# Second sweep of a hybrid GLA/MLA encoder layer: the gated output turned by VectorE and DMA, and a float32 state product

## The chip, the cores and the metric

The kernel runs on one core of a Trainium2 chip. A core has five engines that work side by side, each through its own queue in order: TensorE (PE; its weight loads are listed as PEld), VectorE (DVE), ScalarE (ACT), GpSimd (POOL) and SyncE (SP), which issues most of the DMAs. Sixteen DMA engines move the data. The metric is the device time of one execution, in microseconds; before the change the median of three runs is 1285.17 us (1284.21 to 1286.22).

## The reference

One layer over 2048 rows of width 1024, all in float32. The input is projected once; the columns feed a group of gated linear attention (GLA, 4 heads, key width 64, value width 128) and a group of latent attention (MLA, 4 heads). The two outputs (512 + 512) go through one output projection and a residual LayerNorm. What matters here is the GLA group's end:

```python
o_fwd = gla_chunked(q, k, v, log_af, strict=False)
o_bwd = flip(gla_chunked(flip(q), flip(k), flip(v), flip(log_ab), strict=True))
o = rms_norm(o_fwd + o_bwd, norm_g)          # per head, over 128 values
o = o.reshape(B, S, D_GLA).astype(gate.dtype)
return o * jax.nn.silu(gate)
...
return jnp.concatenate([o_a, o_b], axis=-1) @ w_out
```

In chunked form a chunk's output is a part within the chunk plus the decayed queries times a state that runs over the chunks: `o = o_intra + q_dec @ state`. The forward state runs up through the chunks, the backward one down.

## The kernel before

The rows are cut into 16 chunks of 128. Three stages follow one another.

The first sweep (`sweep_a`) goes from the last chunk to the first. It projects q, k, v and the decays, and computes per chunk the part within the chunk, the decayed queries of both directions stacked on 128 partitions (64 forward, 64 backward), the state update of the forward direction and the finished state of the backward one. Four tiles per chunk go to memory: `qd_s` (queries), `oi_s` (part within the chunk), `su_s` (forward update in partitions 0 to 63, backward state in 64 to 127) and `u_s` (the SiLU gate). From its fifth chunk on, this sweep turns q and k by VectorE in 32x32 blocks and by four DMAs each (`turn`, L824 to L827); its first chunks turn them on TensorE.

The second sweep (`sweep_c`) goes from the first chunk to the last in 8 steps of two chunks. It makes the MLA projections (`ipm`, `pz`, `pq`, `pqr`) and finishes the GLA output. For each chunk it loads the four tiles (`c_lS`, `c_lq`, `c_lo`, `c_lu`; tiles SU, qdb, oib, ub), carries the forward state `Sf` along on GpSimd (`c_Sf1`, `c_Sf2`) and puts the decayed forward state into the lower half of SU (`c_M`), so that one product of contraction 128 adds both directions. That product (`c_Ob`) is written with split operands: ScalarE rounds qdb and SU to fp32r (`c_qhb`, `c_MMh`), GpSimd forms the rests (`c_qlb`, `c_MMl`), and TensorE multiplies, per head, the queries' high part by both parts of the state (256 columns, L1465) and their low part by the state's high part (128 columns, L1466). VectorE adds the second half of that result to oib (`c_oia`) and both to the first (`c_oib`). ScalarE squares, VectorE forms the scale of the norm and multiplies by it and by the gate (`c_og`). TensorE turns the four heads (`c_ot`), ScalarE takes them out of PSUM with the norm's weight as a scale per partition (`c_oT`, gn_c), and SP stores the chunk to `oa_s` (`c_soT`), 128 partitions of 2 KB.

Attention and the output projection come last (`attention`, `OutProj`). Attention goes over 16 pairs of a head and a block of 512 queries. The eight row blocks of w_out are loaded to `raw`, rounded on ScalarE (`split_hi`, L1875) and their rests formed on GpSimd (`split_lo`); the first four blocks, which multiply the GLA half, are handled in blocks 9 to 12 of attention.

The order of the second sweep is written out by hand: `PLACE_C` gives each operation a place in units of one step (two values where the even and the odd chunk of a step differ), with own tables for the first and the last step. Operations are sorted by it, and each engine, SP included, goes through its own in that order (`in_order`). A tile with `bufs=2` has two buffers; who writes the third waits for the readers of the first. DMAs are readers too. The pool `tr` holds PSUM tiles for transposes, of which `ot`, `tm`, `pqr` and `tq` take turns in two buffers; `gp` holds those of `Ob`, `pz` and `pq`.

Of the kernel before, what the change touches and what calls it, by code (L numbers as in the profile page):

```python
# [18 lines left out]
P = 128  # L19
S = 2048  # L20
D = 1024
NK = D // P
NCH = S // P
H = 4
# [106 lines left out]
STEP_C = ("gm1", "gm2", "gm3", "gm4", "sgm", "pq", "qah", "qal", "sqa", "sqr")  # L131
CHUNK_C = ("lx", "xh", "xl", "lS", "lq", "lo", "lu", "sqm", "ssm", "rml", "rmd", "cq", "ckv", "krf", "krfa",
    "krsh", "krsl", "vh", "vl", "tm", "cqTh", "cqTl", "ckvTh", "ckvTl", "krT", "pqr", "qrf", "qrfa",
    "tq", "qrTh", "qrTl", "Sf1", "Sf2", "M", "qhb", "qlb", "MMh", "MMl", "Ob", "oia", "oib", "sqO",
    "ss", "rgl", "rgd", "og", "ot", "oT", "soT")

FETCH_C = ("lx", "xh", "xl")

# [12 lines left out]
    qhb=(-0.048, 0.321),  # L151
    MMh=(-0.034, 0.412),
    sqO=(0.272, 0.988),
    rgl=(0.283, 1.029),
    sqm=(0.14, 0.858),
# [11 lines left out]
    oia=(0.235, 0.863),  # L167
    ss=(0.278, 1.005),
    rgd=(0.359, 1.067),
    og=(0.391, 1.102),  # L170
# [11 lines left out]
    qlb=(-0.043, 0.428),  # L182
    MMl=(0.004, 0.597),
    krfa=(0.262, 0.862),
    krsl=(0.456, 1.044),
    vl=(0.859, 1.227),
# [38 lines left out]
    Ob=(0.066, 0.896),  # L225
    tm=(0.445, 1.143),
    pqr=(0.716, 1.336),
    tq=(1.11, 1.512),
    ot=(1.009, 1.378),
    xh=(-0.3, 1.403),  # L230
    qhb=(-0.513, 0.421),
    MMh=(-0.164, 0.444),
    sqO=(0.469, 0.999),
    rgl=(0.603, 1.027),
    sqm=(0.073, 0.865),
# [11 lines left out]
    oia=(0.316, 0.899),  # L247
    ss=(0.596, 1.015),
    rgd=(0.636, 1.064),
    og=(0.804, 1.171),  # L250
# [11 lines left out]
    qlb=(-0.023, 0.63),  # L262
    MMl=(-0.109, 0.558),
    krfa=(-0.119, 0.94),
    krsl=(0.252, 1.09),
    vl=(0.627, 1.365),
# [24 lines left out]
    Ob=(0.0, 0.299),  # L291
    tm=(0.495, 1.083),
    pqr=(0.749, 1.284),
    tq=(0.919, 2.161),
    ot=(0.915, 1.082),
    xh=(-0.262, -0.109),
    qhb=(-0.096, 0.079),
    MMh=(-0.13, 0.094),
    sqO=(0.15, 0.374),
    rgl=(0.229, 0.457),  # L300
    sqm=(0.101, 0.657),
# [11 lines left out]
    oia=(0.01, 0.311),  # L313
    ss=(0.166, 0.454),
    rgd=(0.332, 0.461),
    og=(0.336, 0.508),
# [11 lines left out]
    qlb=(-0.062, 0.166),  # L328
    MMl=(-0.068, 0.195),
    krfa=(0.255, 0.636),  # L330
    krsl=(0.395, 0.879),
    vl=(0.968, 2.242),
# [6 lines left out]
    soT=(1.09, 2.304),  # L339
# [21 lines left out]
class K:  # L361
# [765 lines left out]
    def sweep_c(self):  # L1127


        with ExitStack() as ctx:  # L1130
            self.w1 = ctx.enter_context(self.tc.tile_pool(name="wk2", bufs=1, reuse_waits="tile"))
            self.sm = ctx.enter_context(self.tc.tile_pool(name="smc", bufs=2, reuse_waits="tile"))
            chunks = [dict(c=c, j=c % 2, st=c // 2) for c in range(NCH)]
            steps = [dict(st=st, ch=chunks[2 * st:2 * st + 2]) for st in range(NCH // 2)]
            for d in chunks:
                d["step"] = steps[d["st"]]
            Sf = self.w1.tile([64, H, P], F32, tag="Sf", name="Sf", bufs=2)
            self.nc.vector.memset(Sf, 0.0)
            self.Sf = Sf
            todo = []  # L1140

            def put(n, st, fn, *a, j=None):
                last = st == len(steps) - 1
                p = PLACE_C[n]
                p = (last and PLACE_C_LAST.get(n)) or (not st and PLACE_C_FIRST.get(n)) or p
                todo.append((st + (p if j is None else p[j]), len(todo), fn, a))

            for n in SETUP_C:
                put(n, 0, getattr(self, "su_" + n))
            for s in steps:  # L1150
                for n in range(8):
                    put("pz", s["st"], self.c_pz, s, n, j=n)
                for n in STEP_C:
                    put(n, s["st"], getattr(self, "c_" + n), s)
            for d in chunks:
                for n in range(4):
                    put("ip" + "abcd"[n], d["st"], self.c_ip, d, n, j=d["j"])
                for n in CHUNK_C:
                    if (d["st"] or n not in FETCH_C) and (d["c"] < NCH - 1 or n not in ("Sf1", "Sf2")):
                        put(n, d["st"], getattr(self, "c_" + n), d, j=d["j"])  # L1160
            last = dict(self.tail)
            for _, _, fn, a in sorted(todo, key=lambda e: e[:2]):
                with self.in_order(last):
                    fn(*a)


    def su_lset(self):
        nc, ins, w1 = self.nc, self.ins, self.w1
        self.gq = self.bc.tile([P, 2], F32, name="gq")
        self.gkv_b = w1.tile([P, H, P], F32, tag="oT", name="gkv_b")[:, 0]  # L1170
# [259 lines left out]
    def c_Sf1(self, d):  # L1430

        d["Sf"], self.Sf = self.Sf, self.w1.tile([64, H, P], F32, tag="Sf", name=f"Sf{d['c']}", bufs=2)
        cw = self.cw[0:64, d["c"]]
        self.nc.gpsimd.tensor_tensor(self.Sf, d["Sf"], cw[:, 2, :, None].to_broadcast([64, H, P]), ALU.mult)

    def c_Sf2(self, d):
        self.nc.gpsimd.tensor_tensor(self.Sf, self.Sf, d["SU"][0:64], ALU.add)

    def c_M(self, d):

        cw = self.cw[0:64, d["c"]]
        self.nc.gpsimd.tensor_tensor(d["SU"][0:64], d.get("Sf", self.Sf), cw[:, 0, :, None].to_broadcast([64, H, P]),
                                     ALU.mult)

    def c_qhb(self, d):
        d["qh"] = self.w1.tile([P, H, P], F32R, tag="qhb", name=f"qhb{d['c']}")
        self.hi(d["qh"], d["qdb"])

    def c_qlb(self, d):
        d["ql"] = self.w1.tile([P, H, P], F32R, tag="qlb", name=f"qlb{d['c']}")  # L1450
        self.lo(d["ql"], d["qdb"], d["qh"], "pool")

    def c_MMh(self, d):
        d["MM"] = self.w1.tile([P, 2, H, P], F32R, tag="MMb", name=f"MMb{d['c']}")
        self.hi(d["MM"][:, 0], d["SU"])

    def c_MMl(self, d):
        self.lo(d["MM"][:, 1], d["SU"], d["MM"][:, 0], "pool")

    def c_Ob(self, d):  # L1460
        mm = self.nc.tensor.matmul
        t = self.gp.tile([P, H, 2, P], F32, tag="gp", name=f"Ob{d['c']}")
        d["Ob"], d["Ob1"], d["rp"] = t[:, :, 0], t[:, :, 1], t[:, 0, 1]
        for h in range(H):
            mm(t[:, h], d["qh"][:, h], d["MM"][:, :, h], start=True, stop=False)  # L1465
            mm(t[:, h, 0], d["ql"][:, h], d["MM"][:, 0, h], start=False, stop=True)  # L1466

    def c_oia(self, d):
        self.nc.vector.tensor_tensor(d["oib"], d["Ob1"], d["oib"], ALU.add)

    def c_oib(self, d):
        self.nc.vector.tensor_tensor(d["Ob"], d["Ob"], d["oib"], ALU.add)
# [19 lines left out]
            self.nc.vector.scalar_tensor_tensor(d["og"][:, h], d["Ob"][:, h], d["rg"][:, h:h + 1], d["ub"][:, h],  # L1492
                                                ALU.mult, ALU.mult)

    def c_ot(self, d):
        d["ot"] = self.tr.tile([P, H, P], F32, tag="tr", name=f"ot{d['c']}")
        for h in range(H):
            self.nc.tensor.transpose(d["ot"][:, h], d["og"][:, h], self.ident)

    def c_oT(self, d):  # L1500
        d["oT"] = self.w1.tile([P, H, P], F32, tag="oT", name=f"oT{d['c']}")
        self.nc.scalar.activation(d["oT"], d["ot"], AF.Copy, scale=self.gn_c[:, 0:1])

    def c_soT(self, d):
        self.nc.sync.dma_start(self.oa_s[d["c"]], d["oT"])

    def rope(self, dst, src, c, n):

# [342 lines left out]
class OutProj:  # L1851
# [211 lines left out]
```

## Time and profile before

| | |
|---|---|
| median of the runs shown | 1285.17 us (1284.21 to 1286.22) |
| profiled execution, own time | 1286.1 us |
| its span | 1284.3 us |
| TensorE clock granted over the span | 0.998 |
| matmuls | 7050 |
| the four transposes of `ot` | 64 in all, from 385.8 to 590.6 us |
| matmuls of `Ob` | 128 in all, from 369.0 to 570.9 us |
| DMA queue of SP (q1) | 127584 packets, 151.86 MB, 38.4% of 16 engines' span |

Times within the profile count from the start of the span. A row of the chain of waits gives a start, a length and what ran; a row of a group gives line, engine, operation, result <- operands, shapes, count, then busy time and mean ns of one, then the engine's idle time just before it and what ended most of that. A line can be that of a helper (L371 rounds, L377 forms a rest, L425 to L427 are a split product).

### The profile page before, as it was taken

Reading aid. Unit: us, or ns where it says so; the run is one execution under the profiler, and the core shown is the slowest. Engines: PE = TensorE matmul, PEld = TensorE weight load, DVE = VectorE, ACT = ScalarE, POOL = GpSimd, SP = SyncE. Lnnn points to the kernel's source line nnn. Section 1 sums busy time; section 2 is a strip of 40 time slices with the busy share of each in tenths; the row PEclk is TensorE's granted clock in tenths of the full one; section 3 lists DMA queues with packets and bytes.
Section 4 is the critical chain, followed back from the end, with each engine's and each line's share of the span. In section 5 each row is a group of like instructions: output and inputs, shape, how many; then the busy total and the mean of one; then the engine's idle time right before and its main releaser. Section 6 shows DMA issues by size and latency. Waiting matters only on the chain.

```text
span 1284.3 us, 19837 instructions
## 1 busy us (share of the span) xinstructions
PE 1259.7 (98%) x7050; PEld 1109.9 (86%) x7050; DVE 899.4 (70%) x1602; ACT 755.5 (59%) x1230; POOL 761.1 (59%) x476
## 2 busy tenths in 40 slices
PE   7999999999999999999999999999999999999997
PEld 7999999999889999999788888888888888887886
DVE  6635554544575555554888888888888888479997
ACT  7544343444565655555788888888888888511110
POOL 0132323222367666650498888889999999944541
PEclk9999999999999999999999999999999999999999
DMA  8223444444755666547201111111133110375752
GB/s 293 78 79 108 115 111 114 115 105 126 255 171 184 205 205 210 194 149 228 76 1 42 41 42 50 46 54 58 58 89 93 41 42 9 123 227 193 220 189 99
DMA packets 135746, 155.25 MB, mean 121 GB/s; under 512 B 43510, under 2 KB 86142, under 8 KB 135648
## 3 DMA queue, kind: packets, MB, share of 16 engines
q1 hardware_dynamic: 127584, 151.86, 38.4%
q0 software_dynamic: 672, 2.10, 0.4%
q8 instruction: 56, 0.92, 0.4%
q10 hardware_dynamic: 7392, 0.03, 0.3%
q14 instruction: 42, 0.34, 0.2%
HBM read 100.43 MB, written 53.51 MB: 120 GB/s over the span
## 4 chain that ended last, share of the span: by engine, by line
PE 82%; DMA 5%; DVE 4%; ACT 2%; issue 2%; POOL 2%; SPq 2%; DVEq 0%; POOLq 0%; ACTq 0%
PE pz L1237 6%; PE ipm L1308 5%; PE o L425 4%; PE o L426 4%; PE o L427 4%; PE pS L1569 4%; PE pS L1570 4%; PE pS L1572 4%; PE pS L1571 4%; PE pS L1573 4%; PE ipa L425 4%; PE ipa L427 4%; PE ipa L426 4%; PE ipg L427 2%; PE ipg L425 2%
## 5 line engine op out<-in xcount | busy, mean ns | idle before, releaser
L377 POOL TENSOR_TENSOR pl<-s,ph 128x1024 fp32r<-128x1024 f32 x128 | 306.4, 2411 | 57.7 <-ACT ph L371 53.8
L1591 DVE TENSOR_TENSOR rm<-pS,rm 128x512 f32<-128x512 f32 x210 | 144.8, 689 | 36.7 <-ACT s L1578 31.5
L1578 ACT ACTIVATE s<-pS 128x1024 f32<-128x1024 f32 x128 | 131.2, 1026 | 61.8 <-PE pS L1573 52.0
L1615 DVE TENSOR_TENSOR s<-s,mb 128x1024 f32<-128x1024 f32 x128 | 151.2, 1212 | 8.9 <-PE mb L1609 8.2
L371 ACT ACTIVATE ph<-s 128x1024 fp32r<-128x1024 f32 x128 | 135.1, 1057 | 16.9 <-PE o L427 16.4
L1619 ACT ACTIVATE s<-s 128x1024 f32<-128x1024 f32 x128 | 131.4, 1050 | 12.2 <-DVE s L1615 12.1
L425 PE MATMUL ipa<-wah,xah 128*128 128x384 f32 (+1 forms) x384 | 129.7, 338 | 5.5 <-ACT wah L371 5.5
L426 PE MATMUL ipa<-wal,xah 128*128 128x384 f32 (+1 forms) x384 | 124.5, 324 | 0.5 <-DVE wal L377 0.5
L427 PE MATMUL ipa<-wah,xal 128*128 128x384 f32 (+1 forms) x384 | 124.4, 324 | 0.0
L1569 PE MATMUL pS<-qh,ckvT_h 128*128 128x512 f32 x256 | 102.7, 401 | 2.0 <-ACT s L1578 1.2
L1072 POOL TENSOR_TENSOR Sb<-Sb,Us 64x512 f32<-64x512 f32 x15 | 20.9, 1394 | 136.9 <-DVE Us L1064 127.8
L425 PE MATMUL o<-ph,vh 128*128 128x512 f32 x256 | 101.0, 395 | 0.0
L1570 PE MATMUL pS<-ql,ckvT_h 128*128 128x512 f32 x256 | 100.0, 391 | 0.0
L1572 PE MATMUL pS<-rh,krs 128*128 128x512 f32 x256 | 99.9, 390 | 0.0
L1571 PE MATMUL pS<-qh,ckvT_l 128*128 128x512 f32 x256 | 99.9, 390 | 0.0
L1573 PE MATMUL pS<-rl,krs 128*128 128x512 f32 x256 | 99.8, 390 | 0.0
L427 PE MATMUL o<-ph,vl 128*128 128x512 f32 x256 | 99.7, 389 | 0.0
L426 PE MATMUL o<-pl,vh 128*128 128x512 f32 x256 | 99.6, 389 | 0.0
L1642 DVE TENSOR_TENSOR ap<-ap,s 128x512 f32<-128x512 f32 x120 | 83.1, 693 | 2.7 <-ACT s L1619 0.7
L377 POOL TENSOR_TENSOR xal<-xaf,xah 128x1024 fp32r<-128x1024 f32 x12 | 29.7, 2477 | 87.8 <-ACT xah L371 87.8
L377 POOL TENSOR_TENSOR ol<-of,oh 128x512 fp32r<-128x512 f32 x32 | 43.2, 1352 | 62.6 <-ACT oh L371 61.9
L425 PEld LDWEIGHTS ipa<-wah,xah 128*128 128x128 f32 x384 | 72.9, 190 | 7.8 <-ACT wah L371 5.5
(308 smaller groups left out, 3595.6 us busy)
## 6 DMA issues: line engine op xcount, KB each, us to landing
xcf<-xT_dram SPq DMA_DIRECT2D x16, 512.0 KB, 5.1
xr<-x_dram SPq DMA_DIRECT2D x16, 512.0 KB, 6.4
out_dram<-rr SPq DMA_DIRECT2D x32, 256.0 KB, 2.2
xaf<-xT_dram SPq DMA_DIRECT2D x14, 512.0 KB, 4.2
oib<-oi_s SPq DMA_DIRECT2D x16, 256.0 KB, 4.0
qdb<-qd_s SPq DMA_DIRECT2D x16, 256.0 KB, 4.0
SU<-su_s SPq DMA_DIRECT2D x16, 256.0 KB, 4.1
ub<-u_s SPq DMA_DIRECT2D x16, 256.0 KB, 4.2
```

What stands on the lines that cost most here:

```text
L371: return nc.scalar.activation(dst, src, AF.Copy).ins
L377: return e.tensor_tensor(dst, src, hi.bitcast(F32), ALU.subtract).ins
L425: mm(out, ah, bh, start=start, stop=False)
L426: mm(out, ah, bl, start=False, stop=False)
L427: mm(out, al, bh, start=False, stop=stop)
L1569: mm(ps[:, e], kh, qh, start=True, stop=False)
L1570: mm(ps[:, e], kh, ql, start=False, stop=False)
L1571: mm(ps[:, e], kl, qh, start=False, stop=False)
L1572: mm(ps[:, e], kr, rh, start=False, stop=False)
L1573: mm(ps[:, e], kr, rl, start=False, stop=True)
L1591: V.tensor_tensor(d["rm"], src[:, e], d["rm"], ALU.max)
L1615: V.tensor_tensor(s, s, d["mb"][:, None, :].to_broadcast([P, 2, QB]), ALU.subtract)
```

## The change

All of it stands in the second sweep, but for one line in the output projection.

- The state product takes qdb and SU as they are, in float32: four matmuls of 128 columns per chunk. The rounding and the rests (`c_qhb`, `c_qlb`, `c_MMh`, `c_MMl`) and the add `c_oia` are gone.
- The gated output is turned by VectorE in 32x32 blocks straight behind `c_og` (`c_oT`); `c_ot` is gone, and so is ScalarE's eviction. Four DMAs per chunk put the blocks in their places in `oa_s`, each from 32 partitions in runs of 32 values. oT has two buffers instead of one.
- The norm's weight moves from that eviction to w_out: ScalarE scales the first four raw blocks in place.
- The state tile is not cleared: chunk 0 copies its update on GpSimd and clears the lower half of its SU there.
- In the tables, oT moves from (0.998, 1.347) to (0.392, 1.103) in the steady steps, and the odd chunk's store from 1.736 to 1.45. In the last step the store keeps its places.

```diff
@@ PLACE_C @@
-    ot=(0.926, 1.312),
...
-    oT=(0.998, 1.347),
+    oT=(0.392, 1.103),
...
-    soT=(1.119, 1.736),
+    soT=(1.119, 1.45),
@@ PLACE_C_FIRST @@
-    oT=(1.14, 1.433),
+    oT=(0.805, 1.172),
...
-    soT=(1.342, 1.538),
+    soT=(1.342, 1.45),
@@ PLACE_C_LAST @@
-    oT=(1.011, 1.153),
+    oT=(0.337, 0.509),
@@ sweep_c @@
-            Sf = self.w1.tile([64, H, P], F32, tag="Sf", name="Sf", bufs=2)
-            self.nc.vector.memset(Sf, 0.0)
-            self.Sf = Sf
+            self.Sf = None
@@ c_Sf1, c_Sf2, c_M @@
-        self.nc.gpsimd.tensor_tensor(self.Sf, d["Sf"], cw[:, 2, :, None].to_broadcast([64, H, P]), ALU.mult)
+        if d["c"]:
+            self.nc.gpsimd.tensor_tensor(self.Sf, d["Sf"], cw[:, 2, :, None].to_broadcast([64, H, P]), ALU.mult)
...
-        self.nc.gpsimd.tensor_tensor(self.Sf, self.Sf, d["SU"][0:64], ALU.add)
+        if d["c"]:
+            self.nc.gpsimd.tensor_tensor(self.Sf, self.Sf, d["SU"][0:64], ALU.add)
+        else:
+            self.nc.gpsimd.tensor_copy(self.Sf, d["SU"][0:64])
...
+        if not d["c"]:
+            return self.nc.gpsimd.memset(d["SU"][0:64], 0.0)
@@ c_qhb, c_qlb, c_MMh, c_MMl, c_oia, c_ot: removed @@
@@ c_Ob @@
-        t = self.gp.tile([P, H, 2, P], F32, tag="gp", name=f"Ob{d['c']}")
-        d["Ob"], d["Ob1"], d["rp"] = t[:, :, 0], t[:, :, 1], t[:, 0, 1]
+        t = self.gp.tile([P, 2, H, P], F32, tag="gp", name=f"Ob{d['c']}")
+        d["Ob"], d["rp"] = t[:, 0], t[:, 1, 0]
         for h in range(H):
-            mm(t[:, h], d["qh"][:, h], d["MM"][:, :, h], start=True, stop=False)
-            mm(t[:, h, 0], d["ql"][:, h], d["MM"][:, 0, h], start=False, stop=True)
+            self.nc.tensor.matmul(t[:, 0, h], d["qdb"][:, h], d["SU"][:, h], start=True, stop=True)
@@ c_oT @@
-        d["oT"] = self.w1.tile([P, H, P], F32, tag="oT", name=f"oT{d['c']}")
-        self.nc.scalar.activation(d["oT"], d["ot"], AF.Copy, scale=self.gn_c[:, 0:1])
+        f2 = lambda t: t.rearrange("p h t -> p (h t)")
+        d["oT"] = self.w1.tile([P, H, P], F32, tag="oT", name=f"oT{d['c']}", bufs=2)
+        self.nc.vector.transpose(f2(d["oT"]), f2(d["og"]))
@@ c_soT @@
-        self.nc.sync.dma_start(self.oa_s[d["c"]], d["oT"])
+        t = d["oT"].rearrange("p h (a t) -> p h a t", a=4)
+        dst = self.oa_s[d["c"]].rearrange("(a r) h (b t) -> b r h a t", a=4, b=4)
+        for b in range(4):
+            self.nc.sync.dma_start(dst[b], t[32 * b:32 * b + 32])
@@ OutProj.split_hi @@
         wh = self.w_tile("h", k)
+        if k < NK // 2:
+            self.nc.scalar.activation(self.raw[k], self.raw[k], AF.Copy, scale=self.k.gn_c[:, 0:1])
         self.k.hi(wh, self.raw[k])
```

More of the change, by code (lines that the diff above doesn't have):

```diff
@@ L133 @@
     "krsh", "krsl", "vh", "vl", "tm", "cqTh", "cqTl", "ckvTh", "ckvTl", "krT", "pqr", "qrf", "qrfa",
-    "tq", "qrTh", "qrTl", "Sf1", "Sf2", "M", "qhb", "qlb", "MMh", "MMl", "Ob", "oia", "oib", "sqO",
-    "ss", "rgl", "rgd", "og", "ot", "oT", "soT")
+    "tq", "qrTh", "qrTl", "Sf1", "Sf2", "M", "Ob", "oib", "sqO",
+    "ss", "rgl", "rgd", "og", "oT", "soT")
 FETCH_C = ("lx", "xh", "xl")
@@ L181 @@
     Sf2=(-0.48, 0.285),
-    qlb=(-0.043, 0.428),
-    MMl=(0.004, 0.597),
     krfa=(0.262, 0.862),
@@ L261 @@
     Sf2=(-0.613, -0.022),
-    qlb=(-0.023, 0.63),
-    MMl=(-0.109, 0.558),
     krfa=(-0.119, 0.94),
@@ L327 @@
     Sf2=(-0.624, 1.82),
-    qlb=(-0.062, 0.166),
-    MMl=(-0.068, 0.195),
     krfa=(0.255, 0.636),
@@ L1169, in su_lset @@
         self.gq = self.bc.tile([P, 2], F32, name="gq")
-        self.gkv_b = w1.tile([P, H, P], F32, tag="oT", name="gkv_b")[:, 0]
+        self.gkv_b = w1.tile([P, H, P], F32, tag="oT", name="gkv_b", bufs=2)[:, 0]
         t1 = w1.tile([P, 2, 512], F32, tag="qa", name="wkr")
@@ L1493, in c_og @@
                                                 ALU.mult, ALU.mult)
[L1495 to L1498, printed above, removed]
     def c_oT(self, d):
-        d["oT"] = self.w1.tile([P, H, P], F32, tag="oT", name=f"oT{d['c']}")
-        self.nc.scalar.activation(d["oT"], d["ot"], AF.Copy, scale=self.gn_c[:, 0:1])
+        f2 = lambda t: t.rearrange("p h t -> p (h t)")
+        d["oT"] = self.w1.tile([P, H, P], F32, tag="oT", name=f"oT{d['c']}", bufs=2)
+        self.nc.vector.transpose(f2(d["oT"]), f2(d["og"]))
     def c_soT(self, d):
-        self.nc.sync.dma_start(self.oa_s[d["c"]], d["oT"])
+        t = d["oT"].rearrange("p h (a t) -> p h a t", a=4)
+        dst = self.oa_s[d["c"]].rearrange("(a r) h (b t) -> b r h a t", a=4, b=4)
+        for b in range(4):
+            self.nc.sync.dma_start(dst[b], t[32 * b:32 * b + 32])
     def rope(self, dst, src, c, n):
```

25 lines of the change are left out of this document (removed).

## The prediction

> **What bounds the kernel now.** The page comes first: which engine is busy, and which one the chain that ended last runs through.
>
> ```profile
> span 1284.3 us, 19837 instructions
> PE 1259.7 (98%) x7050; PEld 1109.9 (86%) x7050; DVE 899.4 (70%) x1602; ACT 755.5 (59%) x1230; POOL 761.1 (59%) x476
> PE 82%; DMA 5%; DVE 4%; ACT 2%; issue 2%; POOL 2%; SPq 2%; DVEq 0%; POOLq 0%; ACTq 0%
> ```
>
> TensorE sets the time, but an average hides where it does not. So the second view cuts the span into stretches: 400 to 550 us is the second sweep in its steady steps, 600 to 610 the turn into attention, 650 to 1070 attention; the short one lies in the first sweep, where only 128-byte runs are being stored.
>
> ```profile
> core 0: us, PE busy (x) PEld busy (x) DVE busy (x) ACT busy (x) POOL busy (x), PEclk, DMA share, GB/s
> 325.00:326.00 1.00, 1.00 (x15) 0.78 (x14) 0.00 (x0) 0.97 (x2) 0.00 (x0) 1.00 0.36 52
> 400.00:550.00 150.00, 150.00 (x1101) 145.61 (x1100) 78.00 (x281) 88.01 (x231) 101.53 (x103) 1.00 0.58 194
> 600.00:610.00 10.00, 10.00 (x45) 8.28 (x45) 5.98 (x8) 4.79 (x5) 0.00 (x0) 1.00 0.91 286
> 650.00:1070.00 420.00, 420.00 (x1931) 347.52 (x1930) 365.61 (x488) 348.04 (x376) 376.13 (x165) 1.00 0.19 50
> ```
>
> In the steady second sweep TensorE is busy all 150 us, while VectorE, ScalarE and GpSimd work 78, 88 and 102. A matmul's listed duration overlaps the next one's, so "busy" does not price an instruction. The chain of waits does, because it gives each matmul only the time until the next could follow. Third view, then: the chain around one chunk (start, length, what), and the same group one step later.
>
> ```profile
> 412.86 0.12 PE Ob L1465
> 412.98 0.06 PE Ob L1466
> 413.04 0.17 PE Ob L1465
> ...
> 413.67 0.06 PE Ob L1466
> 413.73 1.28 PE ipm L1308 x6
> 415.01 0.44 PE ot L1498 x4
> ...
> 444.57 0.44 PE ot L1498 x4
> ```
>
> The state product (8 matmuls) holds TensorE from 412.86 to 413.73, 0.87 us; the four transposes hold it 0.44. A step of two chunks takes 444.57 - 415.01 = 29.56 us, and nothing but TensorE stands in it. Fourth, what TensorE does wait for from 355 to 640 us (total, times, longest):
>
> ```profile
> PE pS L1569 <- ACT s L1578: 1.2, 1, 1.2
> ...
> PE pqr L425 <- ACT oT L1502: 0.8, 1, 0.8
> PE Ob L1466 <- POOL qlb L377: 0.5, 1, 0.5
> PE tq L1401 <- POOL qrf L1396: 0.3, 1, 0.3
> ```
>
> All four lie in the first step, the last step or the turn into attention, none in a steady step.
>
> **The change, part by part.** *Transposes off TensorE.* 16 chunks x 0.44 = 7.0 us leave the engine that sets the time.
>
> *The float32 product.* It takes 4 matmuls per chunk, 128 columns each. The first sweep has this very shape, written as 4 matmuls and carried out as 8 instructions:
>
> ```profile
> 242.82 0.89 PE Up L1061 x8
> 248.59 0.89 PE Op L1047 x8
> ```
>
> So 0.89 replaces 0.87: 16 x 0.02 = +0.3 us. Bounds: +/-0.05 a chunk for the change of operand kind at the edges, +/-0.8 in all. The Trainium skill, page "FP8 and Floating Point Precision", section "TensorE Precision Notes", speaks against this edit: true float32 takes four passes through the array. By that count alone the product streams 4 x 4 x 128 = 2048 columns where the old one streamed 4 x (256 + 128) = 1536, and 0.87 us would become 1.16, taking 4.6 us of the gain away. The two rows agree with four passes (0.89 us / 16 passes of 128 columns = 56 ns); it is the old group that ran slower than its columns, and the measured 0.89 decides.
>
> *Work taken from and given to the other engines.* Per chunk:
>
> ```profile
> L377 POOL TENSOR_TENSOR qlb<-qdb,qhb 128x512 fp32r<-128x512 f32 x16 | 20.6, 1288 | 6.2 <-ACT qhb L371 6.2
> L377 POOL TENSOR_TENSOR MMb<-SU,MMb 128x512 fp32r<-128x512 f32 x16 | 20.6, 1285 | 0.1
> L371 ACT ACTIVATE qhb<-qdb 128x512 fp32r<-128x512 f32 x16 | 9.9, 619 | 0.4 <-POOL Sf L1434 0.3
> L371 ACT ACTIVATE MMb<-SU 128x512 fp32r<-128x512 f32 x16 | 9.9, 621 | 2.9 <-POOL SU L1442 2.9
> L1502 ACT ACTIVATE oT<-ot,gn_c 128x512 f32<-128x512 f32 x16 | 10.8, 676 | 5.2 <-PE ot L1498 5.1 <-DMA oa_s<-oT 0.2
> L1469 DVE TENSOR_TENSOR oib<-Ob,oib 128x512 f32<-128x512 f32 x16 | 11.0, 686 | 1.6 <-PE Ob L1466 1.6
> L824 DVE STREAM_TRANSPOSE qx<-ipa x12: 435/450/451, 87.0 to 322.5; 128x256 f32<-128x256 f32 x12
> ```
>
> GpSimd loses 1.29 + 1.29 = 2.6 us, ScalarE 0.62 + 0.62 + 0.68 = 1.9. VectorE loses one 0.69 us add and gains a block transpose of 512 columns, which lies between 0.45 (the 256-column one) and 0.90 (twice that); I take 0.7, so VectorE stays as it was. None of this is path in a steady step: it frees time under TensorE's 29.56. Chunk 0's copy and clearing stand where two multiplies and an add stood, and the clearing of Sf leaves VectorE: nothing, under the same cover.
>
> It shows only where TensorE waited for this work. The waits for qlb (0.5) and, behind a full GpSimd, for qrf (0.3) in the first step should go: -0.8, bounds 0 and -0.8. The last step's pqr wait for the eviction of ot (0.8) goes with ot, but the next product, pq, needs a PSUM tile that VectorE releases barely in time; half is kept, -0.4, bounds 0 and -0.8.
>
> *The scale on the raw w_out tiles.* Four more ScalarE passes over 128x1024 in blocks 9 to 12 of attention.
>
> ```profile
> L371 ACT ACTIVATE woh<-wof 128x1024 fp32r<-128x1024 f32 x8 | 8.4, 1052 | 3.2 <-DMA wof<-wO_dram 3.2
> ```
>
> 1.05 us each, 4.2 in all if nothing hid it; between nothing and 4.2. ScalarE is idle 420 - 348 = 72 us of that stretch, and the woh copy already stands there without TensorE waiting for it: 0.
>
> *Four stores for one.* Per chunk SP issues 4 DMAs of 512 runs of 128 bytes where it issued one of 128 runs of 2 KB. The nearest rows are the first sweep's qx stores, which have this form at half the size (issue min/median/max ns, then time to landing, us):
>
> ```profile
> L827 SPq DMA_DIRECT2D qx_s<-qx x48: 599/610/1207, 87.4 to 324.9; - x48
> DMA to landing us min/median/max: 2.0/2.0/5.0
> L1505 SPq DMA_DIRECT2D oa_s<-oT x16: 319/376/1717, 389.4 to 599.4; - x16
> DMA to landing us min/median/max: 2.0/3.6/5.7
> ```
>
> So about 4 x 0.65 = 2.6 us of SP instead of 0.4, and landed about 2.6 + 2.0 = 4.6 us after the first issue. On the DMA engines: in the short stretch 52 GB/s of such runs cost a 0.36 share, so 256 KB cost 262 KB / 52 GB/s x 0.36 = 1.8 us of all 16, against 262 / 194 x 0.58 = 0.8 for ordinary traffic; two chunks lift the steady share from 0.58 to about 0.65. In a steady step the loads queued behind an odd chunk's stores (su, oi, qd of the chunk three on) start about 2.6 us later; they serve a product some 25 us away. Another new wait is on SP: the load of qd two chunks on now waits for TensorE's product, not GpSimd's split; behind it stand a u load, the even chunk's stores and the gate's store, none needed within the step.
>
> The turn into attention is different. There a chain runs through SP:
>
> ```profile
> 598.73 4.28 DMA gm_s<-gm
> 608.14 4.51 DMA wvf<-wv_dram
> 612.67 0.73 ACT wvf L1734
> ```
>
> ScalarE stands in front of its wvf work until that load lands; behind it wait the evictions of scores, and for those TensorE waits already (the 1.2 us "pS <- ACT s" above). In SP's order 10 DMAs lie between the gate's store and the wvf load, the last chunk's store among them; in the changed order 13. Three more issues are +1.95 us; the runs may hold the rings another 1.0 (1.8 - 0.8), since the DMA share is 0.91 there; or earlier fetches, which now go ahead, may give some back. Bounds 0 and +3.0; I take +2.0.
>
> **The sum**, against the profiled execution's own time of 1286.1 us (its span of 1284.3 and 1.8 around it): -7.0 + 0.3 - 0.8 - 0.4 + 0 + 2.0 = -5.9, which gives 1280.2. The median of the runs shown, 1285.17, lies 0.9 lower, so I predict **1279.3 us**. With the bounds: at best 0.8 + 0.4 + 2.0 = 3.2 lower, at worst 0.8 + 1.2 + 1.0 = 3.0 higher, 1276.1 to 1282.3.
>
> **The rivals.**
>
> *VectorE held by the stores (slower).* oT has two tiles, so the transpose of chunk c waits until the four stores of c-2 have landed, and all of VectorE's queue waits behind it: rope, the query's low parts, the next product's eviction. The tightest place is an even chunk:
>
> ```profile
> 424.74 1.13 DVE L1492 SCALAR_TENSOR_TENSOR og<-Ob,rg_r,ub 128x128 f32<-128x128 f32 x4
> 426.77 0.48 DVE L1517 TENSOR_TENSOR rope<-pqr,sin 128x128 f32<-128x128 f32 x2
> 427.45 0.73 POOL L1396 TENSOR_TENSOR qrf<-qrf,rope 128x256 f32<-128x256 f32 x1
> 430.30 0.38 PE L1401 MATMUL tq<-ident,qrf 128*128 128x128 f32 x2
> ```
>
> SP reaches chunk 2's stores once the product of chunk 3 has ended (413.73) and two loads are issued, about 414.6; chunk 4's transpose is due at 424.74 + 1.13 = 425.9. So 11.3 us from first issue to landing are free. TensorE's tq has 430.30 - 428.18 = 2.1 more, so from 13.4 us on each excess microsecond costs TensorE one, in 7 even chunks. Slower by over 0.2% needs -5.9 + 7 x (L - 13.4) above 2.6, so L over 14.6; at L = 16 the time is 1297.5. Against it: 4.6 by the rows, 8 with the longest landing. 6%.
>
> *The runs crawl.* If a store's runs did not spread over the 16 DMA engines, a chunk's would take 16 x 1.8 = 29 us on one, longer than half a step; the stores alone would need 16 x 29 = 460 us where the sweep has 8 x 29.56 = 236, and the time would be about 1286 + 224 = 1510. Against it: the qx stores land after 2.0 us. 1%. The Trainium skill, page "VectorE: DVE Perf Modes", section "The three transpose paths", warns of such a loss for a plain DMA that transposes by strides (19 times slower than its transpose hardware, when the innermost stride of the destination is large), and its rules turn 128x128 on TensorE; by its factor a chunk's store would take 19 x 3.6 = 68 us. Here the runs stay 128 bytes long, and the qx row does not bear the factor out.
>
> *Another engine becomes the bound.* TensorE's freed time turns into waits and the steps keep 29.56: 1286.1 - 1.2 + 2.0, or 1286.0 beside the median. Against it: 48 to 72 us idle per 150 on the others, and two of them get less work. 5%.
>
> *The w_out scale shows in full.* +4.2: 1283.5. For it: VectorE and GpSimd are busy 366 and 376 of 420 there, and GpSimd's split waits for ScalarE's copy. Against it: the idle 72 us. 6%.
>
> **How the numbers follow.** The forecast has 82%, the rivals 6, 1, 5 and 6. About 0.2% (2.6 us) is what a measurement can tell from no change, so faster means below 1282.6: the forecast's 82 less 2 for its upper edge, 80%. Same: those 2, the scale's 6, 3 of the third rival's 5, 11%. Slower: 6 + 1 + 2 = 9%. For eight in ten the forecast's own range is stretched a little, down for a turn that gains, up to take in the scale: 1275.5 to 1284.
>
> **What would show it.** Right: the step shorter by 0.84 us (28.7), the product's group at 0.89 in the chain, no waits for qlb or oT, four store issues near 0.6 us each, wvf's load issued about 2 us later behind the gate's store, and TensorE's wait for score evictions grown to about 3. Wrong: VectorE waiting for oa_s at oT; a TensorE wait inside a steady step; TensorE waiting in blocks 9 to 12; or a product group far from 0.89.

## The result, and the profile after

The changed kernel takes 1277.45 us, the median of four runs (1276.64 to 1278.99); the kernel before, beside it, 1285.49. The ratio is 0.994, with a 95% interval of 0.9924 to 0.9956: faster by 8.0 us. The prediction said 1279.3, with a range of 1275.5 to 1284. The profiled execution takes 1277.05 us.

The page of the changed kernel (span, busy time, shares of the chain that ended last):

```profile
span 1275.3 us, 19650 instructions
PE 1251.5 (98%) x6986; PEld 1103.4 (87%) x6986; DVE 898.4 (70%) x1601; ACT 732.4 (57%) x1186; POOL 720.1 (56%) x443
PE 84%; DVE 5%; DMA 4%; ACT 2%; issue 2%; SPq 2%; POOL 0%; DVEq 0%; ACTq 0%; POOLq 0%
```

TensorE still sets the time, with 8 us less work. VectorE is where it was (898 us): it lost the add and gained the block transpose. ScalarE and GpSimd lost 23 and 41 us, which is worth nothing by itself. By stretches, changed kernel:

```profile
400.00:550.00 150.00, 150.00 (x1089) 145.99 (x1088) 78.30 (x283) 75.30 (x207) 77.66 (x82) 1.00 0.71 203
600.00:610.00 10.00, 10.00 (x46) 8.12 (x44) 6.44 (x10) 5.24 (x6) 0.38 (x1) 1.00 0.98 293
650.00:1070.00 420.00, 420.00 (x1932) 347.78 (x1931) 365.06 (x488) 351.67 (x379) 377.67 (x164) 1.00 0.19 50
```

In the steady steps TensorE has no gap, as before; the DMA share has gone from 0.58 to 0.71. From 600 to 610 us it is 0.98 where it was 0.91, but these ten us begin 1.3 us behind the gate's last store before and 9.4 us behind it now. The chain of waits of the changed kernel:

```profile
408.99 0.89 PE Ob L1435 x8
409.88 4.86 PE ipm L1288 x24
414.74 0.22 PE tq L1381 x2
414.95 0.89 PE Ob L1435 x8
...
437.53 0.89 PE Ob L1435 x8
```

The float32 product holds TensorE 0.89 us, and a step takes 437.53 - 408.99 = 28.54 us instead of 29.56. What TensorE waits for in the changed kernel, from 355 to 640 us:

```profile
PE Ob L1435 <- DVE og L1458: 2.1, 1, 2.1
PE mx L1562 <- DVE rm L1556: 1.3, 1, 1.3
PE mb L1574 <- DVE mc L1567: 0.8, 1, 0.8
PE pqr L409 <- DVE cqT_l L359: 0.4, 1, 0.4
```

The four waits shown of before (for s, oT, qlb and qrf) are gone, and two new ones of over 1 us are there: 2.1 us in the last step and 1.3 in the turn. In place of the 0.8 us for oT, the same product pqr now waits 0.4 for cqT_l. The block transpose and the stores, each by its line (ns min/median/max, first and last start):

```profile
L1464 DVE STREAM_TRANSPOSE oT<-og x16: 711/712/715, 376.7 to 572.9; 128x512 f32<-128x512 f32 x16
```

```profile
L1470 SPq DMA_DIRECT2D oa_s<-oT x64: 573/631/1042, 384.1 to 593.7; - x64
DMA to landing us min/median/max: 2.2/3.3/5.9
```

To see where the time went, the second sweep is cut at four starts: TensorE's first matmul of the sweep (ipm), its transposes tm of chunk 2 and of chunk 12, the gate's last store on SP, and the first mb of attention. In the timeline of before, then of the changed kernel:

```profile
355.05 0.36 PE L1308 MATMUL ipm<-wmh,xch 128*128 128x448 f32 x1
403.83 0.27 PE L1361 MATMUL tm<-ident,cq 128*128 128x128 f32 x1
551.63 0.27 PE L1361 MATMUL tm<-ident,cq 128*128 128x128 f32 x1
598.73 0.56 SPq L1258 DMA_DIRECT2D gm_s<-gm  x1
621.62 0.32 PE L1609 MATMUL mb<-ident,mc 128*128 128x128 f32 x1 [0.79 <-DVE mc L1602]
```

```profile
355.19 0.36 PE L1288 MATMUL ipm<-wmh,xch 128*128 128x448 f32 x1
399.95 0.27 PE L1341 MATMUL tm<-ident,cq 128*128 128x128 f32 x1
542.65 0.27 PE L1341 MATMUL tm<-ident,cq 128*128 128x128 f32 x1
590.60 0.58 SPq L1238 DMA_DIRECT2D gm_s<-gm  x1
612.93 0.32 PE L1574 MATMUL mb<-ident,mc 128*128 128x128 f32 x1 [0.78 <-DVE mc L1567]
```

The prediction's terms, laid on the same cuts (2, 10 and 4 of the 16 sets of transposes lie in the first three):

| stretch | before | changed | difference | predicted |
|---|---|---|---|---|
| first step (ipm to tm of chunk 2) | 48.78 | 44.76 | -4.02 | -1.6 |
| five steps (to tm of chunk 12) | 147.80 | 142.70 | -5.10 | -4.2 |
| last stretch (to the gate's store) | 47.10 | 47.95 | +0.85 | -2.1 |
| turn (to the first mb) | 22.89 | 22.33 | -0.56 | +2.0 |
| all the rest | 1017.7 | 1017.5 | -0.2 | 0 |

By the profiles the change brought 9.0 us, 7.7 to 8 by the medians, where 5.9 were summed. Three terms are off by 2.4 to 3 us each, two of them for the better and one for the worse, so they partly cancel: that the time came so near the forecast is in part luck. The experiments look for what is behind each.

### The profile page after: what moved, and what is told of

Same layout as the page of the kernel before. It is cut to its first block, busy times and chain, and to the rows that moved or that the text cites. A ratio compares the mean times of both kernels' runs of the same rounds, so it can differ in the third digit from the quotient of the medians.

```text
span 1275.3 us, 19650 instructions
## 1 busy us (share of the span) xinstructions
PE 1251.5 (98%) x6986; PEld 1103.4 (87%) x6986; DVE 898.4 (70%) x1601; ACT 732.4 (57%) x1186; POOL 720.1 (56%) x443
## 4 chain that ended last, share of the span: by engine, by line
PE 84%; DVE 5%; DMA 4%; ACT 2%; issue 2%; SPq 2%; POOL 0%; DVEq 0%; ACTq 0%; POOLq 0%
PE pz L1217 7%; PE ipm L1288 5%; PE o L407 4%; PE o L408 4%; PE o L409 4%; PE pS L1534 4%; PE pS L1536 4%; PE pS L1537 4%; PE pS L1538 4%; PE pS L1535 4%; PE ipa L407 4%; PE ipa L409 4%; PE ipa L408 4%; PE ipg L407 2%; PE ipg L408 2%; PE ipg L409 2%
```

## The experiments

All are edits of the changed kernel, except "before, without the clearing", which is one of the kernel before. The stretches are read from one profile each, with the cuts above; "last" ends at the gate's store. The kernel before, timed beside the three sets, had medians of 1285.02, 1285.74 and 1285.41.

| kernel | median us | first | one step | last | turn |
|---|---|---|---|---|---|
| before | 1285.4 | 48.78 | 29.56 | 47.10 | 22.89 |
| changed | 1277.45 | 44.76 | 28.54 | 47.95 | 22.33 |
| changed, again | 1279.02 | 44.77 | 28.54 | 47.05 | 22.33 |
| transposes back on TensorE | 1284.02 | 45.65 | 29.50 | 49.68 | 22.02 |
| split product back | 1279.55 | 45.55 | 28.89 | 46.92 | 22.34 |
| clearing back | 1280.39 | 46.49 | 28.54 | 47.96 | 22.33 |
| before, without the clearing | 1282.68 | 46.07 | 29.56 | 47.13 | 22.02 |
| loads of the last step earlier | 1276.51 | 44.76 | 28.54 | 45.35 | 22.33 |
| one store | 1275.61 | 44.76 | 28.54 | 48.63 | 21.37 |
| no scale on w_out | 1278.04 | 44.76 | 28.54 | 47.89 | 22.33 |
| two block transposes | 1278.30 | 45.47 | 28.54 | 49.46 | 21.37 |
| value weights early | 1277.32 | 44.76 | 28.54 | 47.54 | 22.57 |
| loads and value weights | 1274.84 | 44.76 | 28.54 | 45.36 | 21.37 |

Two sets of the same changed kernel differ by 1.6 us in their medians, so smaller differences are read from the stretches, which repeat within 0.1 us but for the last one (47.05 and 47.95). What lies outside the four stretches is 1017.5 us in one profile of the changed kernel and 1021.5 in the other, so single profiles must not be compared by their whole span. In six of the profiles the granted clock fell for some us in the last stretch or in the turn (see the last section); the kernel without the scale, with such a fall, has 47.89 in its last stretch, the changed kernel, without one, 47.95.

**The transposes alone.** TensorE turns again, ScalarE takes the result out, one store per chunk.

```diff
+    def c_ot(self, d):
+        d["ot"] = self.tr.tile([P, H, P], F32, tag="tr", name=f"ot{d['c']}")
+        for h in range(H):
+            self.nc.tensor.transpose(d["ot"][:, h], d["og"][:, h], self.ident)
...
-        self.nc.vector.transpose(f2(d["oT"]), f2(d["og"]))
+        self.nc.scalar.activation(d["oT"], d["ot"], AF.Copy, scale=self.gn_c[:, 0:1])
```

> The changed kernel with the turn undone: four TensorE transposes per chunk into PSUM, the scaled copy by ScalarE, one store per chunk at its old place; the float32 state product and the rest stay. The scale on the raw output weights stays too, so the output is scaled twice by the gain. Theory: each chunk gets its 0.44 us on TensorE back: steady step 28.54 to 29.4, sixteen chunks 7.0 us, plus 0.5 to 0.8 us in the last step where TensorE waited for the scaled copy: +7 to +8, 1284 to 1285. Rival: part of the gain of the steady step (1.02 instead of the 0.88 of the transposes) came with them: step 29.55, +8.5.

The time is 1284.02, 5.0 to 6.6 us above the two sets of the changed kernel, a little less than the 7 to 8 expected, and the step 29.50. So two sets of transposes cost a step 0.96, or 0.48 each, a little more than the 0.44 they hold TensorE: in the listing of before the 24 down-projection matmuls that they stand among take 1.28 + 3.71 = 4.99 us, and undivided 4.86. The remaining 29.56 - 29.50 = 0.06 per step is all that the product brings in a steady step. In the last stretch TensorE's Ob waits 2.3 us here too, so that stall is not the block transpose's; its 49.68 us also hold a fall of the granted clock (0.90 from 560 to 570, 0.93 from 570 to 580).

**The product alone.** The split comes back (two roundings on ScalarE, two rests on GpSimd, the add on VectorE, eight matmuls).

```diff
-            self.nc.tensor.matmul(t[:, 0, h], d["qdb"][:, h], d["SU"][:, h], start=True, stop=True)
+            mm(t[:, h], d["qh"][:, h], d["MM"][:, :, h], start=True, stop=False)
+            mm(t[:, h, 0], d["ql"][:, h], d["MM"][:, 0, h], start=False, stop=True)
...
+        self.nc.vector.tensor_tensor(d["oib"], d["Ob1"], d["oib"], ALU.add)
```

> The changed kernel with the state product undone: float32 operands split in high and low parts by ScalarE and GpSimd, four pairs of one-pass matmuls per chunk, the sum of the correction on VectorE. Turn by VectorE and DMA as in the changed kernel, state tile not cleared. Theory: the early waits of TensorE that left the first step were the split's (product for the low query 0.6, query transposes for their rotation 0.5, low part of x 1.2 us, all behind GpSimd), and 0.15 us of the steady step is the split's too: first step (first down-projection matmul to chunk 4's transposes) 44.8 to about 47, steady step 28.54 to about 28.7, and the last step's stall of 2.1 us is away, since the query buffer is free again before TensorE's product: last step 47.8 to about 45.5. Net +0.6 us (1277 to 1279). Rival: the low part of x was late for another reason (the clearing of the state tile on VectorE) and the steady 0.15 us came with the transposes: first step 45.4, steady 28.5, time 1275.

(By the count of their groups in the trace, the transposes that end the first step are chunk 2's, not chunk 4's, and the last stretch starts at chunk 12's.) The first step is 45.55, not 47: the theory of the early waits falls, the rival holds there. The steady step is 28.89, 0.35 more, above both expectations (four of the five are 28.81 to 28.91, the fifth 29.11). The timeline of TensorE in a steady step shows part of it, first with the split, then in the changed kernel:

```profile
503.35 0.27 PE L1356 MATMUL tm<-ident,krs 128*128 128x128 f32 x1
503.55 0.36 PE L1232 MATMUL pz<-xch,wzh 128*128 128x256 f32 x1
```

```profile
501.63 0.27 PE L1341 MATMUL tm<-ident,krs 128*128 128x128 f32 x1
501.66 0.36 PE L1217 MATMUL pz<-xch,wzh 128*128 128x256 f32 x1
```

The gate product follows 0.20 us behind the transpose instead of 0.03; where the trace names the wait, it is for VectorE's gated output, whose PSUM tile it needs. VectorE's rows of the same moment, with the split and in the changed kernel:

```profile
502.27 1.12 DVE L1493 SCALAR_TENSOR_TENSOR og<-Ob,rg_r,ub 128x128 f32<-128x128 f32 x4
```

```profile
499.64 1.13 DVE L1458 SCALAR_TENSOR_TENSOR og<-Ob,rg_r,ub 128x128 f32<-128x128 f32 x4
```

With the split the gated output is finished at 503.39, 0.16 us before the gate product; in the changed kernel at 500.77, 0.89 before it. The old add (0.69) stands ahead of the gated output, between the state product and it; the block transpose stands behind it, and made twice (below) it does not lengthen the step. So the two edits help each other, but not by room on VectorE: without its transposes TensorE comes to the gate product earlier, and without the split and its add the tile is free by then. No run takes the add out alone, so this rests on the rows. The last stretch has no stall of Ob, as the theory said, but is 46.92 and not 45.5.

**The clearing of the state tile.** It was costed at nothing. One kernel puts it back, another takes only it out of the kernel before.

```diff
-            self.Sf = None
+            Sf = self.w1.tile([64, H, P], F32, tag="Sf", name="Sf", bufs=2)
+            self.nc.vector.memset(Sf, 0.0)
+            self.Sf = Sf
```

> The changed kernel with the clearing of the state tile back on VectorE ahead of the sweep, and with GpSimd's scaled copy and sum for chunk 0 as before. Theory: the wait of TensorE of 1.2 us for the low part of x in the first step was behind the clearing on VectorE: first step 44.8 to 45.9, time +1.2. Rival: it came from the split of the query and state on GpSimd and ScalarE, whose turns shift VectorE's: time as the changed kernel, within 0.5.

> The kernel before, with only the clearing of the state tile taken off VectorE (chunk 0 copies its update and clears its half on GpSimd, as in the changed kernel). Theory: the wait of TensorE for the low part of x, 1.2 us, goes: first step (first down-projection matmul to chunk 2's transposes) 48.8 to 47 to 47.6, time 1.2 to 1.8 us less than before. Rival: with the split's work on GpSimd still there, another wait takes its place, and the first step stays at 48.4 to 48.8.

Both theories hold, and the size is larger than expected: +1.73 us in the first step with the clearing back, -2.71 (48.78 to 46.07) with it alone gone, -2.7 in the median too (ratio 0.9977, 0.9968 to 0.9986). The kernels of the table lead from one end to the other: 48.78, without the clearing 46.07, with the float32 product as well 45.65, without TensorE's transposes as well 44.76. In the kernel before, TensorE's wait is this row, which stands second among the waits that the prediction quotes from:

```profile
PE ipm L1308 <- DVE xcl L377: 1.2, 1, 1.2
```

VectorE's timeline of the kernel before shows the mechanism, and the kernel without the clearing what is left (the bracket is idle time before an instruction, and what ended it):

```profile
352.53 0.48 DVE L1138 MEMSET Sf<- 64x512 f32 x1 [2.93 <-DMA oi_s<-oi]
352.94 2.65 DVE L377 TENSOR_TENSOR wml<-wmr,wmh 128x448 fp32r<-128x448 f32 x3
355.50 2.35 DVE L377 TENSOR_TENSOR xcl<-xcf,xch 128x1024 fp32r<-128x1024 f32 x2
```

```profile
346.40 4.93 DVE L377 TENSOR_TENSOR wml<-wmr,wmh 128x448 fp32r<-128x448 f32 x7
351.24 1.22 DVE L377 TENSOR_TENSOR xcl<-xcf,xch 128x1024 fp32r<-128x1024 f32 x1
```

The clearing takes 0.48 us, but VectorE stands idle 2.93 us in front of it until a store of the first sweep has landed (that Sf takes over the memory of the stored tile is inferred). Behind it lie the low parts of weights and of x, and TensorE waits for those. In the kernel before without the clearing, the waits for qlb and qrf are gone as well, with the split still in place. In the kernel with the clearing back, the granted clock fell to 0.83 in two stretches of ten us, from 560 and from 610, so its median and what lies behind the sweep say less than its first step.

**The new stall of the last step.** VectorE and SP of the changed kernel where TensorE's Ob of chunk 15 waits:

```profile
559.74 0.70 DVE L1438 TENSOR_TENSOR Ob<-Ob,oib 128x512 f32<-128x512 f32 x1 [3.72 <-DMA oib<-oi_s]
```

```profile
543.38 9.55 SPq L1396 DMA_DIRECT2D qdb<-qd_s  x2
553.03 0.38 SPq L1396 DMA_DIRECT2D SU<-su_s  x1
...
555.46 1.05 SPq L1396 DMA_DIRECT2D oib<-oi_s  x2
```

VectorE stands 3.72 us for the correction of chunk 14, with chunk 13's gated output behind it in its queue. That correction's load was issued late: SP was held between two query loads: by the single records of the row at 543.38 the first, by the table's order chunk 15's, goes out at once and the second, chunk 14's, only at 552.61, behind TensorE's product of chunk 13 (551.53 to 552.58), which now reads the buffer that it takes. Before, GpSimd's split had freed that buffer earlier. The edit moves chunk 14's two loads ahead of chunk 15's query, which then is the one that waits.

```diff
 PLACE_C_LAST
-    lq=(-0.287, -0.357),
-    lo=(-0.124, 0.045),
+    lq=(-0.4, -0.357),
+    lo=(-0.39, 0.045),
```

> The changed kernel with two loads of the last step issued earlier: the query and the correction of chunk 14 go ahead of the load of chunk 15's query, which waits for TensorE's state product of chunk 13. Theory: the stall of TensorE of 2.1 us in the last step (its product of chunk 15 waits for VectorE, and VectorE stood 3.72 us for the correction of chunk 14, whose load lay behind the waiting query load) goes. The stretch from the last step's transposes of the down-projection (the even chunk's tm) to the gate's store, 47.78 us, shrinks to 45.3 to 46, and the time falls by 1.8 to 2.5 us against the changed kernel, to about 1275. Rival: VectorE's own queue is the limit there and the wait only changes its name: no more than 0.5 us.

The timelines of SP and of VectorE in this kernel:

```profile
535.79 0.43 SPq L1396 DMA_DIRECT2D qdb<-qd_s  x1
536.33 0.38 SPq L1396 DMA_DIRECT2D oib<-oi_s  x1
...
552.15 0.33 SPq L1396 DMA_DIRECT2D qdb<-qd_s  x1
```

```profile
556.70 0.70 DVE L1438 TENSOR_TENSOR Ob<-Ob,oib 128x512 f32<-128x512 f32 x1 [1.14 <-DMA rl_s<-qrTl]
```

The correction's load is issued at 536.33 and chunk 15's query waits until 552.15, VectorE's add comes right after TensorE's product, the Ob wait is gone and the last stretch falls from 47.95 to 45.35. The theory holds for the stretch; the median, 1276.51, is 0.9 to 2.5 us below the two sets of the changed kernel.

**The turn into attention.** Two kernels ask what the stores cost there. One issues a plain store, the other fixes the order of ScalarE's passes on the value weights, which no table of the kernel sets.

```diff
-            self.nc.sync.dma_start(dst[b], t[32 * b:32 * b + 32])
+        self.nc.sync.dma_start(self.oa_s[d["c"]], d["oT"])
```

> The changed kernel with one plain store per chunk (128 partitions of 2 KB) in place of the four; the blocks of the turned tile are then not put in their places, so the output is another. Theory of the prediction: the three further issues cost SP 1.95 us ahead of the load of the value weights at the turn into attention; without them the turn (gate's store to attention's first mb) gets shorter than the changed kernel's 22.3 us by up to 2, the steady step stays at 28.54. Rival: at the turn the four stores cost nothing, because ScalarE's work on these weights stands two score copies later in its queue in the changed kernel (behind the seventh, before: behind the fifth; with one store it is again behind the fifth): turn 22.3 to 22.9, time within 1 us of the changed kernel.

```diff
+                if (i, j) == (0, 5):
+                    self.tc.add_manual_dep(a, wv_i.name, ..., reason="in_order")
```

> The changed kernel with one order fixed: ScalarE's two passes on the value weights stand behind the fifth score copy of attention's first block, as before the change, where the changed kernel has the first behind the seventh copy and the second behind the eighth. Theory: the load of these weights lands about 4.5 us after its issue, 10.4 us behind the gate's store, so ScalarE stands about 3 us in front of it, TensorE waits 2 to 2.5 us for score copies and the turn grows from 22.3 to 24 to 24.8 us; that is the +2.0 of the prediction, which the other order had avoided. Rival: the turn ends with VectorE's row maximum in either order, and stays at 22.3 to 22.9.

With one store the load of the value weights is issued 8.48 us behind the gate's store, with four 10.37 to 10.41 (11.02 in the kernel with two block transposes). So the three further issues do cost 1.9 us there, and the 9.41 of the profiled kernel before was a late case of one store: in the kernel before without the clearing it is 8.47, with the transposes back 8.55. With one store the turn is 21.37, with four and the same order of ScalarE 22.57: 1.2 us, of which the prediction expected 2. The steady step is the same with one store and four: 28.54. TensorE's wait for score copies in the second kernel:

```profile
PE pS L1534 <- ACT s L1543: 0.9, 1, 0.9
PE mx L1565 <- DVE rm L1559: 0.3, 1, 0.3
```

It is 0.9 and not the 2 to 2.5 expected (ScalarE could start 3.3 us after the load's issue, not 4.5), and the wait for the row maximum has shrunk from 1.3 to 0.3 in exchange. So the turn moved by 0.24 us only; here the rival held. But why did the changed kernel wait 1.3 for the row maximum? Its last row maximum is long. By line, changed kernel (ns min/median/max), and GpSimd's timeline at that moment:

```profile
L1556 DVE TENSOR_TENSOR rm<-s,rm x14: 692/694/1650, 596.0 to 609.8; 128x512 f32<-128x512 f32 x14
```

```profile
609.62 1.27 POOL L359 TENSOR_TENSOR wv_l<-wvf,wv_h 128x512 fp32r<-128x512 f32 x1 [20.59 <-ACT wv_h L353]
```

The last of the 14 starts at 609.8, just behind GpSimd's rest of the value weights, and takes 1.65 us instead of 0.69: it ends at 611.44, 0.55 us after GpSimd has ended at 610.89. The Trainium skill, page "SBUF — State Buffer", section "SBUF: two separate sides", describes such a lock: a VectorE operation with two SBUF inputs and a GpSimd operation that reads SBUF share one pair of ports, and the later one waits for the whole of the other. The two rows agree with that, up to 0.14 us. So do other kernels, in which a row maximum starts later within this GpSimd operation: with one store, with the value weights early and in the kernel before it takes 0.95 to 0.97 us, and it too ends about 0.55 us after GpSimd.

**The scale, and VectorE's room.**

```diff
-        if k < NK // 2:
-            self.nc.scalar.activation(self.raw[k], self.raw[k], AF.Copy, scale=self.k.gn_c[:, 0:1])
```

> The changed kernel without the norm's weight: ScalarE does not scale the raw output weights, so the output lacks that factor. Theory: ScalarE's 4.2 us lie in its idle time in blocks 9 to 12 of attention, time as the changed kernel within 0.5 us. Rival: the scale shows in full, 4 us less.

```diff
         self.nc.vector.transpose(f2(d["oT"]), f2(d["og"]))
+        self.nc.vector.transpose(f2(d["oT"]), f2(d["og"]))
```

> The changed kernel with VectorE's block transpose made twice per chunk (same result): 0.71 us more of VectorE per chunk. Theory: VectorE has room under TensorE's step; steady step 28.54 to 28.7, and only the last step, where TensorE waits for VectorE, gets 0.7 to 1.5 us longer (48 to 49.4): time +0.5 to +2. Rival: TensorE's first gate product of a step waits at the limit for VectorE's gated output (with the split product put back it waited 0.2 us there), so each of the 7 steps gets 0.7 us longer: +5.

Without the scale the span is 1275.5 against 1275.3 and the median between the two sets of the changed kernel: it costs nothing. With the transpose made twice the steady step is 28.54 to the hundredth, so a second 0.71 us behind the gated output fits there. The first step grows by 0.71 (a wait for GpSimd's sum of qrf, 0.4, among it) and the last by 1.5, at the upper end expected. The median lies between the changed kernel's two all the same, since the turn is 0.96 shorter: in this kernel the value weights' passes stand behind the eighth score copy, and GpSimd's rest misses the row maximum.

**Both orders mended.** The last set runs the changed kernel again, and a version with the loads of the last step earlier and ScalarE's passes on the value weights behind the eighth score copy.

```diff
+                if (i, j) == (0, NP - 1):
+                    self.tc.add_manual_dep(wv_i, a.name, ..., reason="in_order")
```

> The changed kernel once more, for a direct comparison with the next: 1276.5 to 1278 us; last stretch (chunk 12's transposes to the gate's store) 47.5 to 48, turn 22.3.

> The changed kernel with two orders altered: chunk 14's query and correction loads ahead of chunk 15's waiting query load, and ScalarE's two passes on the value weights behind the eighth score copy of attention's first block (changed kernel: first behind the seventh, where it delays the last copy by 0.7 us and with it VectorE's row maximum). Theory: last stretch 45.3 us instead of 47.9, turn 21.4 instead of 22.3, together 3 to 3.6 us less than the changed kernel: 1273.5 to 1274.5. Rival: the 1.26 us in which TensorE waits for the row maximum stay, since VectorE sets it: 2.5 us less, turn 22.3.

The version takes 1274.84 us, ratio to before 0.9912 (0.9898 to 0.9925), where the changed kernel beside it has 0.9945 (0.9932 to 0.9958): 4.2 us less, and 3.5 by the stretches of the changed kernel's first profile (2.6 in the last, 0.96 in the turn; 1.7 in the last by its second). What is left for TensorE to wait for, and the row maximum in this version:

```profile
PE mb L1577 <- DVE mc L1570: 0.8, 1, 0.8
PE pqr L409 <- DVE cqT_l L359: 0.4, 1, 0.4
...
PE mx L1565 <- DVE rm L1559: 0.3, 1, 0.3
```

```profile
L1559 DVE TENSOR_TENSOR rm<-s,rm x14: 691/692/693, 594.5 to 608.3; 128x512 f32<-128x512 f32 x14
```

Both stretches came as expected and the time 0.3 us above its range, but the mechanism was not as it was put: in the changed kernel the last copy is not delayed, it starts when TensorE has its scores ready; it is the row maximum behind it that meets GpSimd. With four stores the turn is now 21.37, the same as with one: their 1.9 us on SP cost nothing in this order. The changed kernel's second set is 1.0 us above the range expected, and its last stretch, 47.05, below (TensorE's Ob waits 1.0 us there, not 2.1); its profile has a granted clock of 0.91 from 600 to 620.

## Why the prediction was right

The direction and the main term were right, and the time lay in the range; three smaller terms were off by more than 2 us each. That they partly cancelled is luck: the gain of the first step, which was not foreseen, paid for most of the stall in the last one.

- **Transposes off TensorE, -7.0.** Right. Measured 0.48 a set instead of 0.44, which is 7.7 for 16.
- **The float32 product, +0.3.** The row was right (0.89 us), the sum a little off: with the old transposes in place the step is 0.06 shorter with it, and with the new ones 0.35, since the split's chain then holds up the gate product. The four-pass count did not cost the 4.6 us that the comparison with 1.16 gave.
- **The first step, -0.8.** Mis-sized: without the two sets of transposes it brought 3.1. "The waits for qlb and qrf should go" was true, but they were laid to GpSimd's split, and they go with the clearing alone. The step that failed is "the clearing of Sf leaves VectorE: nothing, under the same cover": it passed over the 2.93 us that VectorE stood in front of it, ahead of the operands TensorE was waiting for, and over the row of TensorE's 1.2 us for xcl. The clearing alone is 2.7 of the 4.0 us.
- **The last step, -0.4, and its transposes.** The wait of pqr for oT (0.8) is gone and one of 0.4 for cqT_l is in its place, so half was kept, as said, though by another wait than the one for pq's tile. What failed is "behind it stand a u load, the even chunk's stores and the gate's store, none needed within the step": that is the steady step's order. In the last step's table the correction of chunk 14 stands behind the waiting load, and TensorE lost 1.0 to 2.1 us to it.
- **The turn, +2.0.** "Three more issues are +1.95 us" was right on SP (1.9). That TensorE's wait for score copies would grow to about 3 was not: ScalarE's passes on the value weights moved behind the seventh copy, and even in the old order it is 0.9. The cost reappeared as the meeting of VectorE and GpSimd, 0.96 us, and the profile taken of before had a long turn, so the difference came out at -0.56; against the 22.02 of the two other kernels with TensorE's transposes and one store it is +0.3. That the runs "may hold the rings another 1.0" shows in no run.
- **VectorE's transpose, 0.7, the stores, 0.65 each, the scale, 0.** Right: 0.712 and 0.631 us, and no time for the scale. The landing was put too early: 4.6 us after the first issue was forecast, and the fourth store of a chunk landed 4.2 to 7.2 us after it (eleven chunks, in which the trace has its landing). The DMA share is 0.71 instead of 0.65.
- **The rivals.** None came. VectorE was not held by the stores (no wait of VectorE for oa_s stands in the trace, and 11.3 us were free), and the 128-byte runs did not crawl; the factor of 19 named there does not show. The steps did not keep their 29.56, and the scale cost nothing.

## What to carry to other kernels

A short operation's price is what it waits for and who stands behind it in its queue: a clearing of 0.48 us cost 1.7 to 2.7 us. When an operand is freed by another engine than before, follow the loads that wait for its buffer in every order table, first and last step too, and list what stands behind them. When two edits are made together, time each without the other: TensorE could use all of the time that the transposes left (0.96 us a step and not 0.67) only because the other edit shortened the chain that feeds its next product.

## What was not expected of the hardware

A VectorE maximum of two SBUF tiles took 1650 ns instead of 692 when a GpSimd operation had started 0.2 us before it. Three other kernels show the same, shorter.

In six of the profiles (changed again, transposes back, clearing back, one store, no scale, two block transposes) the granted clock halved for 3.4 us, once behind the stall in the last step or the one in the turn, and with the clearing back behind both; in ten-us stretches that reads as 0.83 to 0.93. The changed kernel's first profile has stalls of the same size and no fall. The same two us without the scale and in the changed kernel (the third number from the end is the clock):

```profile
564.00:566.00 2.00, 2.00 (x8) 1.82 (x8) 1.84 (x10) 1.46 (x7) 1.81 (x3) 0.50 0.64 96
```

```profile
564.00:566.00 2.00, 1.51 (x9) 0.94 (x8) 1.83 (x11) 1.53 (x7) 1.74 (x3) 1.00 0.61 91
```

The traces tell the two apart. In each trace the changes of the clock lie on a grid of 3.41 us, counted from the clock's first rise. In all thirteen traces, a period of this grid in which no matmul ran for 1.92 us or more in all is followed by a fall (seven times within the kernels, thirteen times at their ends), and one with 1.70 or less never is. The stall of 2.03 us without the scale lies in one period (560.06 to 563.47); the 2.07 us of the changed kernel lie across a border at 560.65, with 1.66 us behind it. This is read from the traces, and no run was made to test it.
